# Issuing the column tiles of TensorE back to back in a two-layer diffusion trunk

## The chip, the cores and the metric

The kernel runs on one core of one Trainium2 chip. The metric is device time in microseconds (us) of one launch; lower is better. Times of a kernel are given as the median of several runs, and one further execution was taken with the hardware profiler.

## What is computed

Two layers of a hybrid trunk over 512 latent tokens and 256 context tokens of width 1024, all in float32. Cut to what matters here:

```python
for l in range(DEPTH):                                   # DEPTH = 2
    mod   = silu(c)     @ w_mod[l] + b_mod[l]            # w_mod[l]: 1024 x 6144, two rows only
    mod_c = silu(c_ctx) @ w_mod[l] + b_mod[l]
    h, hc = modulate(rmsnorm(x), ...), modulate(rmsnorm(ctx), ...)
    # one projection of h and hc; its columns feed two groups of heads:
    #   (A) 8 heads of a bidirectional gated delta rule in chunks of 64, latent scans start
    #       from the final context state; a triangular system is solved for every chunk
    #   (B) 8 heads of latent attention over all latent and all context keys
    y = concat(A, B) @ w_out[l];  x = x + g1 * y
    x = x + g2 * swiglu(modulate(rmsnorm(x), ...))       # hidden width 2816
    # the same for ctx in layer 0
return rmsnorm(x)
```

Attention of group B is `softmax(q k^T) v` for 512 queries and 768 keys per head.

## The kernel before, in words

**Products.** Activations lie transposed, features on the 128 partitions and tokens along the free axis. Large products split every operand into a high and a low float32r half (`load_w`, `split`, `gemm`, L193 to L222): three matmuls of 128x512 for each 128x128 block of weights. The weights of a block are loaded by SyncE's DMA queue, rounded by ScalarE and subtracted by VectorE (L205, L206).

**Column tiles.** Three products have an output of fewer than 128 partitions, so that several of them fit side by side in TensorE's columns:

- *Modulation* (class `Mod`, L257 to L305). `Mod.unit` (L284) takes one block of 128 rows and 2048 columns of `w_mod` in four parts of 512 columns. Part j is multiplied with the two conditioning vectors, padded to 32 columns, into partitions 32j to 32j+31 of the bank `psM` (L290). A layer has 24 units of four matmuls. The first eight of layer 0 run inside `ctx_in` from tiles `g` of 1024 columns; the other sixteen run in `mod_rest(0)`. In layer 1 eight run in `ctx_in1` and sixteen in `mod_rest(1)`, all from tiles `m` of 512 columns, each with a DMA of its own (L270).
- *Values* (`attend`, L945). For a pair of heads and each of six blocks of 128 keys, the scores of head 0 and head 1 are made in a bank `psB` (L956), ScalarE takes the exponential (L961), and L965 multiplies the exponentials by the values of the head into partitions 0 to 63 or 64 to 127 of `psA`.
- *Denominators* (L972), the same with a column of ones, once for a pair of heads.

A float32 matmul shows as two records in the trace, so a unit is eight records of L290 and a value pair four of L965.

**Order of the work.** Eleven kinds of streams, written as Python generators, make the two layers: `ctx_in`, `ctx_mla`, `ctx_ffn`, `ctx_in1`, `ctx_chain` (delta rule of the context), `lat_in`, `lat_chain` (delta rule of the latents, heads 0 to 3 and then 4 to 7), `mla_prep`, `mla_att`, `mod_rest`, `lat_ffn`. `weave` (L78) takes them in turns: a stream yields its estimated length and its work on TensorE and VectorE, `paced` (L1311) multiplies these by a pace, and the stream with the earliest time and the lowest rank is next. Rank and pace of each stream stand in the table `TUNE` (L51). The order that `weave` traces sets priorities; a list scheduler then orders each engine's queue by its own estimate of when inputs are ready, and may put other work between two matmuls that stand together in the source. Each engine runs its queue strictly in that order.

**The delta rule.** `gdn_pre` (L448) solves the triangular systems on VectorE: 31 steps of a product and a subtraction (L566 to L570, seen as L139 with tiles `st` and `g`), after which TensorE joins the blocks (L582, L583, L592, L593). It runs six times: context, latent heads 0 to 3, latent heads 4 to 7, in each layer.

**Maxima.** `prep` (L899) finds the row maxima of the scores of a head with matmuls L928 and L933 and VectorE reductions L929 and L934.

Of the kernel before, what the change touches and what calls it, by code (L numbers as in the profile page):

```python
# [3 lines left out]

# [16 lines left out]
P = 128  # L21
D = 1024
KD = 8
# [25 lines left out]


TUNE = {  # L51
    ("ctx_in", 0): (3, 0.7),
    ("ctx_mla", 0): (1, 0.7),
    ("ctx_ffn", 0): (3, 0.801),
    ("ctx_in1", 0): (3, 1.0),
    ("ctx_chain", 0): (0, 1.0),
    ("mod_rest", 0): (1, 0.7),
    ("lat_in", 0): (2, 1.0),
    ("lat_chain", 0): (1, 1.0),
    ("mla_prep", 0): (4, 1.17),  # L60
    ("mla_att", 0): (5, 0.374),
    ("lat_ffn", 0): (6, 1.0),
    ("ctx_chain", 1): (0, 1.0),
    ("mod_rest", 1): (1, 1.0),
    ("lat_in", 1): (2, 1.0),
    ("lat_chain", 1): (0, 0.6),
    ("mla_prep", 1): (3, 1.5),
    ("mla_att", 1): (5, 1.0),
    ("lat_ffn", 1): (6, 1.0),
}  # L70

# [34 lines left out]
def trunk_kernel(ctx, tc, xin, cc, wmod, small, win, wuq, wuk, wuv, wout, wgu, wdn, cst, rope, out):  # L106
    nc = tc.nc
    V, A, G, PE = nc.vector, nc.scalar, nc.gpsimd, nc.tensor
# [54 lines left out]
    ones_k = cst_t[:, C_ONE:C_ONE + 1]  # L163
# [20 lines left out]
    sc = cp.tile([P, KD, 32], F32, name="sc")  # L184
# [39 lines left out]
    def gemm_f32(w, xs, o):  # L224
        for k, x_ in enumerate(xs):
            PE.matmul(o, w[:, k * P:k * P + P], x_, start=k == 0, stop=k == len(xs) - 1)  # L226

    def pipelined(items, load, use, depth=1):
        items = list(items)
        q = []  # L230
        for i in range(min(depth, len(items))):
            q.append(load(items[i]))
        for i, it in enumerate(items):
            if i + depth < len(items):
                q.append(load(items[i + depth]))
            yield use(it, q.pop(0))
# [20 lines left out]
    class Mod:  # L257
# [26 lines left out]
        def unit(self, g, k, parts):  # L284
            l = self.l
            if k == 0:
                self.ps = ps("M")
            o = self.ps
            for j in range(4):
                PE.matmul(o[32 * j:32 * j + 32, :], sc[:, k, :], parts[j],  # L290
                          start=k == 0, stop=k == KD - 1, tile_position=(0, 32 * j))
            if k < KD - 1:
                return
            rows = slot("t", w=512)
            cpy(rows, o)
            pt = ps("M")
            for i in range(4):
                PE.matmul(pt[:, 8 * i:8 * i + 8], rows[:, P * i:P * i + P], sel, start=True, stop=True)
            o = self.t[:, 16 * g:16 * g + 16, :].rearrange("p (j i) r -> p i j r", j=4)
            b = smalls[l][:, B_MOD + 16 * g:B_MOD + 16 * g + 16].rearrange("p (j i) -> p i j", j=4)  # L300
            tt(o, pt[:, 0:32].rearrange("p (i j r) -> p i j r", i=4, j=4), b.unsqueeze(3).to_broadcast([P, 4, 4, 2]), ADD)
            for i, gg, scale, gain in ((0, 0, 8, N1), (1, 2, 32, N2)):
                if gg == g:
                    ts(self.al[:, i], self.t[:, scale:scale + 8, :], 1.0, op0=ADD)
                    tt(self.al[:, i], self.al[:, i], smalls[l][:, gain:gain + KD].unsqueeze(2).to_broadcast([P, KD, 2]))  # L305
# [417 lines left out]
    v = SimpleNamespace()  # L723
    nrs = [slice(64 * hp, 64 * hp + 64) for hp in range(2)]
# [170 lines left out]
    def mla_lat(l, cqh, kvs, yt):  # L895
# [49 lines left out]
        def attend(j, s, tag):  # L945
            y = raw_tile("f") if j < 3 else slot("hd")
            py = ps(tag)
            acc = [None, None]
            for i in range(6):
                pts = []  # L950
                for hp in range(2):
                    Q, K = s["Q"][hp], s["K"][0 if i < 2 else 1][hp]
                    b = P * (i if i < 2 else i - 2)
                    pst = ps("B")
                    for cnt, (ki, qi) in enumerate(((0, 0), (0, 1), (1, 0))):
                        PE.matmul(pst, K[ki][:, b:b + P], Q[qi], start=cnt == 0, stop=cnt == 2)  # L956
                    if i == 0:
                        acc[hp] = pt = wp.tile([P, 512], F32, name=nm("acc"), tag=("fh", "fl")[hp], bufs=3)
                    else:
                        pt = slot("t", w=n)  # L960
                    act(pt, pst, AF.Exp, scale=scale)  # L961
                    pts.append(pt)
                    yield 0.75, 0.75, 0.1
                for hp in range(2):
                    PE.matmul(py[nrs[hp]], v.vt[i][:, P * j + 64 * hp:P * j + 64 * hp + 64], pts[hp], start=i == 0, stop=i == 5)  # L965
                if i:
                    for hp in range(2):
                        tt(acc[hp], acc[hp], pts[hp], ADD, e=V)
                yield 1.2, 1.2, 0.1
            pd = ps(tag)  # L970
            for hp in range(2):
                PE.matmul(pd[nrs[hp]], ones_k.to_broadcast([P, 64]), acc[hp], start=True, stop=True)  # L972
            den = slot("t", w=n)
            V.reciprocal(out=den, in_=pd)
            stt(y, den, 1.0 / D, py, MUL, MUL)
            yt.append(y)
# [468 lines left out]
```

## Time and profile before

| | |
|---|---|
| median of 3 runs | 2263.81 us (2262.18 to 2264.55) |
| the profiled execution's own time | 2268.44 us |
| its span from the first to the last instruction | 2266.4 us |
| TensorE (PE) busy | 2087.5 us, 92% of the span |
| VectorE (DVE) busy | 1495.9 us, 66% |
| ScalarE (ACT) busy | 872.6 us, 39% |
| mean granted TensorE clock | 0.954 of full speed |

PE and PEld are matmuls and weight loads of TensorE. Matmuls are pipelined, so what one costs in a stream is the distance from its start to the next start and not its duration. The chain of waits is the work that ended last, followed back from the last instruction.

### The profile page before, as it was taken

Reading aid. Unit: us, or ns where it says so; the run is one execution under the profiler, and the core shown is the slowest. Engines: PE = TensorE matmul, PEld = TensorE weight load, DVE = VectorE, ACT = ScalarE, POOL = GpSimd, SP = SyncE. Lnnn points to the kernel's source line nnn. Section 1 sums busy time; section 2 is a strip of 40 time slices with the busy share of each in tenths; the row PEclk is TensorE's granted clock in tenths of the full one; section 3 lists DMA queues with packets and bytes.
Section 4 is the critical chain, followed back from the end, with each engine's and each line's share of the span. In section 5 each row is a group of like instructions: output and inputs, shape, how many; then the busy total and the mean of one; then the engine's idle time right before and its main releaser. Section 6 shows DMA issues by size and latency. Waiting matters only on the chain.

```text
span 2266.4 us, 40584 instructions
## 1 busy us (share of the span) xinstructions
PE 2087.5 (92%) x16048; PEld 1606.8 (71%) x16048; DVE 1495.9 (66%) x2926; ACT 872.6 (39%) x1541; POOL 126.3 (6%) x283
## 2 busy tenths in 40 slices
PE   6999989889899999999999999996985998999996
PEld 3767677789895556778888886675643576888885
DVE  4779659986678667688544457797678455444445
ACT  3453365444344434452332234435332234222333
POOL 0200013000200000010000000200010000000000
PEclk9999988899999999999999999997997999999998
DMA  8335604343345401252222236621110012323332
GB/s 321 134 122 170 210 22 129 112 152 127 108 145 163 127 25 56 71 168 89 89 76 94 93 96 211 191 93 35 38 34 14 30 66 75 95 96 98 98 96 76
DMA packets 130637, 240.41 MB, mean 106 GB/s; under 512 B 15184, under 2 KB 30064, under 8 KB 130448
## 3 DMA queue, kind: packets, MB, share of 16 engines
q1 hardware_dynamic: 124592, 224.10, 30.3%
q0 software_dynamic: 5856, 13.74, 2.2%
q8 instruction: 126, 2.06, 0.4%
q14 instruction: 63, 0.52, 0.1%
HBM read 228.24 MB, written 6.91 MB: 104 GB/s over the span
## 4 chain that ended last, share of the span: by engine, by line
PE 75%; DVE 14%; DMA 4%; ACT 4%; issue 3%; SPq 0%; ACTq 0%; DVEq 0%; POOL 0%
PE psA L221 33%; PE psM L221 14%; PE psF L221 4%; PE psB L956 3%; PE psA L965 3%; PE psM L290 2%; PE psA L226 2%; PE psB L617 2%; DVE g L139 2%; PE psC L664 2%; DVE g L148 1%; DVE fl L139 1%; PE psC L676 1%; PE psC L687 1%; ACT t L151 1%
## 5 line engine op out<-in xcount | busy, mean ns | idle before, releaser
L221 PE MATMUL psA<-hx,wh 128*128 128x512 f32 x1680 | 535.7, 398 | 21.3 <-ACT hx L151 10.8
L151 ACT ACTIVATE wh<-wr 128x512 fp32r<-128x512 f32 (+2 forms) x410 | 249.1, 608 | 642.3 <-PE psA L221 458.4
L139 DVE TENSOR_TENSOR wl<-wr,wh 128x512 fp32r<-128x512 f32 (+2 forms) x410 | 270.5, 660 | 228.8 <-ACT wh L151 228.4
L221 PEld LDWEIGHTS psA<-hx,wh 128*128 128x128 f32 x1680 | 315.1, 190 | 112.6 <-ACT hx L151 14.0
L221 PE MATMUL psA<-hx,wl 128*128 128x512 f32 x840 | 332.3, 396 | 4.4 <-DVE wl L139 4.4
L221 PE MATMUL psM<-hx,wh 128*128 128x512 f32 x704 | 217.5, 390 | 0.0
L221 PEld LDWEIGHTS psA<-hx,wl 128*128 128x128 f32 x840 | 159.6, 190 | 43.2 <-DVE wl L139 6.0
L151 ACT ACTIVATE fh<-fr 128x512 fp32r<-128x512 f32 (+3 forms) x186 | 110.8, 599 | 157.0 <-PE psF L221 47.9
L139 DVE TENSOR_TENSOR fl<-fr,fh 128x512 fp32r<-128x512 f32 (+3 forms) x186 | 119.8, 650 | 53.3 <-ACT fh L151 51.3
L148 DVE SCALAR_TENSOR_TENSOR g<-psA,mod,g 128x512 f32<-128x512 f32 x112 | 83.9, 749 | 103.9 <-PE psA L221 103.3
L221 PEld LDWEIGHTS psM<-hx,wh 128*128 128x128 f32 x704 | 132.3, 188 | 27.3
L221 PE MATMUL psM<-hx,wl 128*128 128x512 f32 x352 | 137.0, 389 | 0.0
L221 PE MATMUL psF<-m,fh 128*128 128x256 f32 x600 | 116.8, 293 | 8.2 <-ACT tc L151 5.4
L221 PE MATMUL psA<-hd,wh 128*128 128x512 f32 x384 | 120.5, 392 | 0.0
L221 PEld LDWEIGHTS psF<-m,fh 128*128 128x128 f32 x600 | 95.9, 195 | 14.6 <-ACT tc L151 7.1
L221 PE MATMUL psA<-ox,wh 128*128 128x512 f32 x320 | 100.7, 393 | 0.0
L221 PE MATMUL psM<-m,fh 128*128 128x256 f32 x416 | 80.5, 291 | 8.0 <-ACT m L151 7.9
L221 PE MATMUL psF<-m,fl 128*128 128x256 f32 x300 | 86.5, 288 | 1.5 <-DVE fl L139 1.5
L151 ACT ACTIVATE t<-psB 128x512 f32<-128x512 f32 x80 | 47.7, 597 | 99.2 <-PE psB L956 74.0
L226 PE MATMUL psA<-m,g 128*128 128x256 f32 x320 | 75.6, 397 | 10.7 <-DMA g<-win 4.0
L221 PEld LDWEIGHTS psA<-hd,wh 128*128 128x128 f32 x384 | 71.7, 188 | 16.5 <-DVE hd L139 1.0
L226 PEld LDWEIGHTS psA<-m,g 128*128 128x128 f32 x320 | 63.2, 200 | 21.3 <-ACT m L151 7.6
(382 smaller groups left out, 3797.6 us busy)
## 6 DMA issues: line engine op xcount, KB each, us to landing
wr<-wgu SPq DMA_DIRECT2D x176, 256.0 KB, 2.6
m<-wmod SPq DMA_DIRECT2D x160, 256.0 KB, 4.1
fr<-wgu SPq DMA_DIRECT2D x88, 256.0 KB, 2.7
wr<-win SPq DMA_DIRECT2D x80, 256.0 KB, 3.0
wr<-wdn SPq DMA_DIRECT2D x64, 256.0 KB, 2.6
g<-win SPq DMA_DIRECT2D x20, 512.0 KB, 7.4
g<-wmod SPq DMA_DIRECT2D x16, 512.0 KB, 10.2
fr<-wdn SPq DMA_DIRECT2D x32, 256.0 KB, 2.8
```

Source lines behind the costliest of these rows:

```text
L139: (e or V).tensor_tensor(out=out, in0=a, in1=b, op=op)
L148: V.scalar_tensor_tensor(out=out, in0=a, scalar=s, in1=b, op0=op0, op1=op1)
L151: A.activation(out, a, f, **kw)
L221: PE.matmul(o, ww[:, wk], xx if n is None else xx[:, a:a + n], start=cnt == 0, stop=cnt == 3 * nk - 1)
L226: PE.matmul(o, w[:, k * P:k * P + P], x_, start=k == 0, stop=k == len(xs) - 1)
L290: PE.matmul(o[32 * j:32 * j + 32, :], sc[:, k, :], parts[j], start=k == 0, stop=k == KD - 1, tile_position=(0, 32 * j))
L617: PE.matmul(pv[s, q, d, :], u3(lh[d])[s, c, :], u3(rh[d])[s, c, :], start=True, stop=True)
L664: PE.matmul(o[s], x_[s], y_[s], start=i == 0, stop=i == len(mm) - 1)
L676: PE.matmul(v4(ws)[s, hi, d, :], v4(w)[s, hi, d, :], S[s, hi, d, :], start=True, stop=True)
L687: PE.matmul(v4(kv)[s, hi, d, :], u3(ks[d])[s, unit(hi, n, d), :], v4(u)[s, hi, d, :], start=True, stop=True)
L956: PE.matmul(pst, K[ki][:, b:b + P], Q[qi], start=cnt == 0, stop=cnt == 2)
L965: PE.matmul(py[nrs[hp]], v.vt[i][:, P * j + 64 * hp:P * j + 64 * hp + 64], pts[hp], start=i == 0, stop=i == 5)
```

## The change

Two things change. A helper `together` makes the matmuls of a group of column tiles from the last to the first, each queued on TensorE directly behind the one made before it. The edge concerns the order in TensorE's queue alone: none of them waits for another to finish. It is used for the modulation units, the value pairs and the denominator pairs. And ten of the eighteen entries of `TUNE` get other numbers, two of these in rank and pace both.

```diff
+    def together(mms):
+        prev = None
+        for mm in mms[::-1]:
+            with nullcontext() if prev is None else tc.issue_after(prev.ins):
+                prev = mm()
...
-            for j in range(4):
-                PE.matmul(o[32 * j:32 * j + 32, :], sc[:, k, :], parts[j],
-                          start=k == 0, stop=k == KD - 1, tile_position=(0, 32 * j))
+            together([partial(PE.matmul, o[32 * j:32 * j + 32, :], sc[:, k, :], parts[j],
+                              start=k == 0, stop=k == KD - 1, tile_position=(0, 32 * j)) for j in range(4)])
...
-                for hp in range(2):
-                    PE.matmul(py[nrs[hp]], v.vt[i][:, P * j + 64 * hp:P * j + 64 * hp + 64], pts[hp], start=i == 0, stop=i == 5)
+                together([partial(PE.matmul, py[nrs[hp]], v.vt[i][:, P * j + 64 * hp:P * j + 64 * hp + 64], pts[hp],
+                                  start=i == 0, stop=i == 5) for hp in range(2)])
...
-            for hp in range(2):
-                PE.matmul(pd[nrs[hp]], ones_k.to_broadcast([P, 64]), acc[hp], start=True, stop=True)
+            together([partial(PE.matmul, pd[nrs[hp]], ones_k.to_broadcast([P, 64]), acc[hp], start=True, stop=True) for hp in range(2)])
...
-    ("ctx_ffn", 0): (3, 0.801),
+    ("ctx_ffn", 0): (3, 1.003),
...
-    ("mla_prep", 1): (3, 1.5),
-    ("mla_att", 1): (5, 1.0),
+    ("mla_prep", 1): (5, 1.755),
+    ("mla_att", 1): (5, 1.07),
```

All matmuls of the three groups stand at L232 in the changed kernel, the line of `prev = mm()`; lines behind it are five or six higher than before. The number of instructions on every engine is the same.

TensorE in `mod_rest(0)`, while the latent projection L221 runs beside it; `psM` is the bank of the modulation, `m` a part of `w_mod`. Before:

```order
188 L290 MATMUL psM_1112<-m_948,sc 32x512
189 L221 MATMUL psA_1207<-hx_676,wl_1126 128x512
190 L221 MATMUL psA_1207<-hx_682,wh_1125 128x512
191 L221 MATMUL psA_1207<-hx_683,wh_1125 128x512
192 L221 MATMUL psA_1207<-hx_682,wl_1126 128x512
193 L290 MATMUL psM_1112<-m_950,sc 32x512
194 L290 MATMUL psM_1112<-m_952,sc 32x512
195 L221 MATMUL psA_1281<-hx_640,wh_1197 128x512
196 L221 MATMUL psA_1281<-hx_641,wh_1197 128x512
197 L290 MATMUL psM_1112<-m_954,sc 32x512
```

And now:

```order
136 L221 MATMUL psA_923<-hx_682,wl_908 128x512
137 L232 MATMUL psM_1020<-m_889,sc 32x512
138 L232 MATMUL psM_1020<-m_887,sc 32x512
139 L232 MATMUL psM_1020<-m_885,sc 32x512
140 L232 MATMUL psM_1020<-m_883,sc 32x512
141 L221 MATMUL psA_1045<-hx_640,wh_913 128x512
```

The four parts of a unit, which stood among projections alone or in twos, follow one another in reversed order.

TensorE in the attention of layer 1, first pair of heads; `psA_16078` before and `psA_16097` now is the output of the values, L956 (now L961) the scores, L478 and L542 (now L483 and L547) work of the delta rule. Before:

```order
6595 L965 MATMUL psA_16078<-t_16590,m_16008 64x512
6596 L941 MATMUL psA_16401<-ident_r,mneg_16399 128x128 x4
6597 L965 MATMUL psA_16078<-t_16596,m_16008 64x512
...
6608 L965 MATMUL psA_16078<-t_16628,m_16014 64x512
6609 L972 MATMUL psA_16675<-acc_16083,cst 64x512
6610 L965 MATMUL psA_16078<-t_16655,m_16014 64x512
6611 L478 MATMUL psB_16681<-cst,g_2746_14771 64x64
6612 L972 MATMUL psA_16675<-acc_16089,cst 64x512
```

And now:

```order
6598 L961 MATMUL psB_16701<-hx_15524,hx_15503 128x512
6599 L536 MATMUL psB_16784<-cst,g_3025_16559 128x2 x8
6600 L547 MATMUL psB_16794<-g_2699_14568 64x64
6601 L232 MATMUL psA_16097<-t_16705,m_16034 64x512
6602 L232 MATMUL psA_16097<-t_16663,m_16034 64x512
6603 L232 MATMUL psA_16724<-acc_16108,cst 64x512
6604 L232 MATMUL psA_16724<-acc_16102,cst 64x512
```

The two heads of a pair stand behind one another, the head whose exponential is made last in front.

VectorE at the end of the sixth triangular solve (layer 1, latent heads 4 to 7); the rows with `st` are steps of the solve, L929 and L934 (now L934 and L939) the maxima. Before:

```order
2463 L929 TENSOR_REDUCE mx_17254<-psA_17264 128x1
2464 L139 TENSOR_TENSOR st_17037<-g_3119_17026,g_3120_17027 128x112
2465 L139 TENSOR_TENSOR g_3120_17027<-g_3120_17027,st_17037 128x4x28
2466 L934 TENSOR_REDUCE mx_17254<-psA_17267 128x2
...
2475 L139 TENSOR_TENSOR g_3120_17027<-g_3120_17027,st_17037 128x31
2476 L573 STREAM_TRANSPOSE g_3118_17025<-g_3120_17027 128x32x32
```

And now:

```order
2459 L139 TENSOR_TENSOR g_3096_16949<-g_3096_16949,st_16959 128x31
2460 L578 STREAM_TRANSPOSE g_3094_16947<-g_3096_16949 128x32x32
2461 L579 STREAM_TRANSPOSE g_3095_16948<-g_3096_16949 128x32x32
2462 L934 TENSOR_REDUCE mx_17270<-psA_17271 128x1
...
2467 L939 TENSOR_REDUCE mx_17270<-psA_17287 128x2
```

The six maxima of the last head, which were spread through the last steps of the solve, follow behind its end, and the solve's last step stands sixteen rows earlier in VectorE's queue.

## Rows read from the trace of the kernel before

**Rows 1.** The page: busy us of the engines, share of the span, count.

```profile
PE 2087.5 (92%) x16048; PEld 1606.8 (71%) x16048; DVE 1495.9 (66%) x2926; ACT 872.6 (39%) x1541; POOL 126.3 (6%) x283
```

**Rows 2.** Chain of waits by line: windows 135:276, 700:760, 748:930, 1370:1446, 1537:1642, 1642:1756, 1756:1872.

```profile
by line: PE psA L221 76.4%; PE psM L290 15.1%; PE psB L542 3.8%; PE psB L531 1.3%; PE psF L330 0.9%; PE psB L370 0.7%; PE psF L221 0.6%; PE psM L298 0.6%; PE psB L417 0.3%; PE psB L397 0.2%; PE psB L399 0.2%; PE psB L398 0.2%
...
by line: PE psM L290 22.5%; PE psA L965 14.7%; PE psA L221 9.2%; PE psB L956 8.8%; DMA fr<-wdn 6.1%; PE psA L928 5.1%; DMA m<-wmod 5.0%; issue 4.6%; PE psA L972 3.3%; DVE st L139 3.2%; DVE g L139 3.2%; DVE hd L139 2.2%; PE psB L582 2.1%; PE
...
by line: PE psA L221 30.1%; PE psB L956 16.5%; PE psA L965 16.5%; PE psB L617 5.1%; PE psC L664 5.0%; PE psA L928 3.3%; PE psA L972 3.3%; PE psC L676 2.7%; PE psC L687 2.0%; PE psA L941 1.9%; DVE t L974 1.9%; DVE mx L934 1.5%; DVE g L139 1.
...
by line: PE psA L221 67.7%; PE psM L290 17.3%; DMA m<-wmod 6.4%; PE psB L330 2.6%; PE psB L370 1.4%; SPq L270 1.2%; PE psM L298 1.0%; issue 0.8%; PE psB L417 0.5%; PE psB L397 0.4%; PE psB L399 0.3%; PE psB L398 0.3%; PE psB L478 0.3%
...
by line: PE psB L956 7.9%; PE psA L965 7.5%; PE psA L928 7.1%; PE psC L664 6.8%; PE psA L221 6.5%; PE psA L779 6.1%; PE psB L617 5.9%; PE psC L676 5.3%; PE psC L687 4.6%; DVE mx L934 3.1%; DVE t L139 3.1%; PE psA L330 3.1%; DVE g L139 2.9%;
...
by line: PE psB L956 14.4%; PE psA L965 9.1%; DVE g L139 7.0%; issue 6.7%; DVE mx L929 5.9%; PE psA L928 4.9%; DVE acc L139 4.8%; DVE mx L934 4.0%; DVE st L139 3.8%; PE psA L941 3.4%; PE psA L972 3.4%; DVE t L974 2.9%; ACT t L151 2.7%; PE p
...
by line: PE psA L221 39.7%; PE psB L956 13.0%; PE psA L965 12.0%; PE psB L617 7.1%; PE psC L664 6.0%; PE psC L676 4.3%; PE psC L687 3.7%; issue 3.1%; PE psC L719 1.8%; PE psC L713 1.8%; PE psA L972 1.7%; PE psB L582 1.3%; PE psB L592 1.2%; 
```

**Rows 3.** Windows: length, busy us (count) of PE, PEld, DVE, ACT, POOL; clock, DMA.

```profile
135.00:276.00 141.00, 141.00 (x769) 97.53 (x769) 113.17 (x244) 49.89 (x94) 6.97 (x29) 0.99 0.57 189
...
748.00:930.00 182.00, 173.61 (x1549) 113.87 (x1550) 120.69 (x218) 72.34 (x130) 4.37 (x15) 0.94 0.19 60
...
1642.00:1756.00 114.00, 81.34 (x491) 45.19 (x490) 94.33 (x191) 34.57 (x59) 12.94 (x15) 0.87 0.08 24
1756.00:1872.00 116.00, 111.04 (x1338) 79.93 (x1338) 60.78 (x110) 36.89 (x61) 0.00 (x0) 0.95 0.14 49
```

**Rows 4.** Timeline of PE near 151 us: start, length, line, output, form, count.

```profile
150.84 1.05 PE L290 MATMUL psM<-m,sc 128*32 128x512 f32 x4
151.82 0.73 PE L221 MATMUL psA<-hx,wh 128*128 128x512 f32 x2
```

**Rows 5.** Timeline of PE near 720 us.

```profile
719.73 0.40 PE L928 MATMUL psA<-hd,hd 128*128 128x512 f32 x1
719.96 0.39 PE L956 MATMUL psB<-hx,hx 128*128 128x512 f32 x1
720.28 1.06 PE L290 MATMUL psM<-m,sc 128*32 128x512 f32 x8
721.28 1.07 PE L965 MATMUL psA<-t,m 128*64 128x512 f32 x2
722.28 0.50 PE L928 MATMUL psA<-hd,hd 128*128 128x512 f32 x1
722.62 0.87 PE L956 MATMUL psB<-hx,hx 128*128 128x512 f32 x3
```

**Rows 6.** Timeline of weight loads (PEld): one whole unit near 246 us.

```profile
246.37 0.16 PEld L290 LDWEIGHTS psM<-m,sc 128*32 128x32 f32 x8 [0.35 <-DVE g L139]
```

**Rows 7.** Timeline of PE at the first eight units; in brackets idle time and its end.

```profile
17.89 1.05 PE L290 MATMUL psM<-g,sc 128*32 128x512 f32 x4 [0.24 <-DMA g<-wmod]
```

**Rows 8.** Chain of waits near 1742 us in order of time: start, length, what.

```profile
1742.12 0.81 PE psA L928
1742.96 0.70 DVE mx L929
1743.70 0.81 PE psA L928
...
1753.24 3.01 issue
```

**Rows 9.** Lines L290, then L965: idle time of TensorE before them, times.

```profile
  DMA m<-wmod: 15.3, 18
...
  ACT t L151: 11.5, 19
```

**Rows 10.** The page: exponentials of the scores on ScalarE; landing of the modulation's parts.

```profile
L151 ACT ACTIVATE t<-psB 128x512 f32<-128x512 f32 x80 | 47.7, 597 | 99.2 <-PE psB L956 74.0
...
m<-wmod SPq DMA_DIRECT2D x160, 256.0 KB, 4.1
```

More of the change, by code (lines that the diff above doesn't have):

```diff
@@ L1 @@
-from contextlib import ExitStack
+from contextlib import ExitStack, nullcontext
 from functools import partial
@@ L51 @@
 TUNE = {
-    ("ctx_in", 0): (3, 0.7),
-    ("ctx_mla", 0): (1, 0.7),
-    ("ctx_ffn", 0): (3, 0.801),
-    ("ctx_in1", 0): (3, 1.0),
+    ("ctx_in", 0): (3, 0.749),
+    ("ctx_mla", 0): (3, 0.7),
+    ("ctx_ffn", 0): (3, 1.003),
+    ("ctx_in1", 0): (2, 1.0),
     ("ctx_chain", 0): (0, 1.0),
     ("mod_rest", 0): (1, 0.7),
-    ("lat_in", 0): (2, 1.0),
+    ("lat_in", 0): (2, 0.595),
     ("lat_chain", 0): (1, 1.0),
-    ("mla_prep", 0): (4, 1.17),
+    ("mla_prep", 0): (4, 1.064),
     ("mla_att", 0): (5, 0.374),
     ("lat_ffn", 0): (6, 1.0),
-    ("ctx_chain", 1): (0, 1.0),
+    ("ctx_chain", 1): (2, 0.85),
     ("mod_rest", 1): (1, 1.0),
-    ("lat_in", 1): (2, 1.0),
+    ("lat_in", 1): (1, 1.0),
     ("lat_chain", 1): (0, 0.6),
-    ("mla_prep", 1): (3, 1.5),
-    ("mla_att", 1): (5, 1.0),
+    ("mla_prep", 1): (5, 1.755),
+    ("mla_att", 1): (5, 1.07),
     ("lat_ffn", 1): (6, 1.0),
```

## The prediction

> **What bounds the kernel now.** I began with the page: TensorE is busy for 2087.5 of 2266.4 us, VectorE for 1495.9 [rows 1]. So TensorE is the bound over the whole, but not everywhere, and the chain of waits says where. From 135 to 276 us all of the chain is TensorE's (the first line of [rows 2]), TensorE is busy for 141.00 of 141.00 us and VectorE for 113.17 [rows 3]: whatever leaves TensorE's queue there shortens the run. From 748 to 930 us it is nearly so, 173.61 of 182 us. In layer 1 between 1642 and 1756 us it is not: VectorE is busy for 94.33 of 114 us and TensorE for 81.34, since the triangular solve, the maxima and the sums of the exponentials share VectorE there (the sixth line of [rows 2]), and the granted clock falls to 0.87 while it is 0.99 in the first stretch [rows 3].
>
> **What a column tile costs.** A lone modulation matmul and a whole unit can be compared directly. One unit's half, four records, starts at 150.84 and the next matmul at 151.82: 0.98 us [rows 4]. A whole unit, eight records, starts at 720.28 and the next at 721.28: 1.00 us [rows 5]. So four column tiles that stand together run in the time of one or two. A value pair's half costs the same 1.00 us (721.28 to 722.28). I call such a run of different column tiles, with nothing between them, a round: it costs 1.0 us, whatever it holds. Beside this, TensorE pays for changing shape: two full-width matmuls start 0.23 us apart (719.73 to 719.96), but 0.32 us pass before a round (719.96 to 720.28) and 0.34 after one (722.28 to 722.62), so about 0.10 us a change.
>
> The page "TensorE: Matmul & The Clock Gate" of the Trainium skill (Part 3, The mechanism) says that a weight load overlaps with matmuls in flight only when its row group differs; column tiles all use the same rows, so by that rule a unit's loads would wait in turn and a group would gain little. The row decides otherwise: the eight loads of a whole unit lie within 0.16 us [rows 6], and by it the sum below stands, where by the rule it would be near nothing.
>
> **What the change removes.** In TensorE's queue before, the 192 modulation matmuls make 69 rounds, the 96 value matmuls 74 and the 16 denominators 9; now 49, 49 and 8. So 152 rounds become 106: 46 fewer at 1.0 us, 46 us. Changes of shape between neighbours in the queue fall from 640 to 585, which is 55 at 0.10 us, 5.5 us. TensorE loses 51.5 us of work, 1.12 us a round. What of it lies on the path goes by place:
>
> - `mod_rest(0)`, 27 rounds to 16: 11 at 1.12 is 12.3 us. It lies in the stretch that is TensorE's alone, and 113 us of VectorE's work fit into the 129 that stay. I count 11, since a unit's last parts must still land.
> - The eight units in `ctx_in1`, 14 to 9: 5.6 us. Around them the modulation is 22.5% of the chain, but landings of `wdn` and `wmod` are 11% (the second line of [rows 2]). I count 4.
> - Values and denominators of layer 0, 38 to 28: 11.2 us. TensorE is busy for 95% of that stretch, and the values are 16.5% of the chain. I count 9.5.
> - `mod_rest(1)`, 20 to 16: 4.5 us, with 6.4% of the chain a wait for `wmod` (the fourth line of [rows 2]). I count 3.
> - Values and denominators of layer 1, 45 to 29: 17.9 us. On the chain are values for 7.5% of 105, 9.1% of 114 and 12.0% of 116 us and denominators for 3.4% of 114 and 1.7% of 116 (the last three lines of [rows 2]): 38 of some 45 us. But where VectorE is the close second a shorter TensorE queue only uncovers it, so I count 0.6 of it, 10.7.
>
> That is 38 us. The first eight units gain nothing: each waits for its DMA [rows 7], and the group now waits for the later of two.
>
> **What the other order moves.** The new table moves little: between the same landmarks (the six solves, the two feed-forward stages) TensorE's and VectorE's queues hold the same work as before but for the rounds. From layer 0's output projection to the start of layer 1 (930 to 1370 us) and from layer 1's output projection to the end nothing changes, so I count 0 there. Two moves matter. The solve of latent heads 0 to 3 in layer 0 starts 32 rows earlier in VectorE's queue and ends six rows later; six rows of about 0.7 us are at most 4 us, and the context's feed-forward covers them while it has TensorE's chain, so 0; without that cover it is 4. In layer 1 the six maxima of the last head go behind the solve. They now alternate with TensorE on the chain, 0.81 and 0.70 us, 1.58 us a step [rows 8], six times, some 9 us in front of the solve's end. Behind it they lie beside the joining of the blocks, where the chain stands for 3.01 us in issue anyway. I count 5 of the 9, for the products behind must wait for the reductions in turn; the bounds are 0 and 9.
>
> Sum: 38 and 5 make 43 us less. The profiled execution's own time was 2268.44, so it would be 2225; the median lies 4.6 us under it, at 2263.81, and so I forecast **2221 us** for the median.
>
> **The rivals.**
>
> *Half of it is hidden.* If VectorE, the DMA landings and the new order eat what TensorE gives back in all places but the two that are TensorE's alone (11 and 9.5 us), 20 us remain: 2244. For it speaks that VectorE is busy for four fifths of 135 to 276 and of 1642 to 1756 us; against it that the chain names the removed lines themselves with 15 to 22% in three of the windows.
>
> *All of it and more.* The full 51.5 us, and 9 us from the maxima, would give 2203. For it speaks that a shorter value stretch also lets the reductions start earlier, since they alternate with it on TensorE.
>
> *Groups wait for their latest input, and the run is slower.* TensorE's queue is strict. A value pair now starts only when both exponentials are there, 0.60 us each on ScalarE, and a unit only when all four parts have landed, 4.1 us each from issue [rows 10]; before, the first part ran while the next was on its way. Everything behind the group waits too. There are 40 units outside the start and 56 value and denominator groups. The 43 us are lost at 0.45 us a group. If each pair waited one exponential (34 us) and each unit 1 us more (40 us), the run would end 31 us later, at 2295. For it speaks that L290 already waits for DMA 15.3 us in 18 times and L965 for exponentials 11.5 us in 19 [rows 9]. Against it: in the new queue score matmuls and delta-rule products stand between the last score of a pair and its values, and the parts are requested a unit ahead.
>
> *The tiles stand together and still take turns.* Then only the order changes: 2264, no change. Against it speak, plainly, [rows 5, 6]. The rule of the Trainium skill named above speaks for it.
>
> **How the numbers follow.** A measurement of this kernel tells about 0.2%, 4.5 us, from no change. I give my forecast, between 2211 and 2236, 0.50; half hidden, 2236 to 2257, 0.22; more than all, under 2211, 0.14; groups that wait, slower by over 4.5 us, 0.08; the tiles in turns, 0.02, and waits that just balance the gain, 0.04. The range that leaves out no more than 2 in 10 goes from 2203, the full sum with 9 us of the maxima, to 2250. Faster is 0.50 and 0.22 and 0.14, that is 0.86; same 0.06; slower 0.08.
>
> **What would show it.** Right: L232 has 49, 49 and 8 rounds that begin together; the busy time of PE falls by about 45 to 50 us; layer 1's output projection starts about 40 us earlier, and the distance from there to the end stays within 2 us of what it is; the stretch with `mod_rest(0)` shortens by about 11 us with PE still busy throughout. Half hidden would show as the same fall of busy time with more idle time on PE, ended by VectorE or DMA. The slower rival would show as waits of L232 for `ACT t` and `DMA m<-wmod` well above the present 27 us together. I would be wrong altogether if records of one group started 0.4 us apart instead of a few ns, or if the stretch between layer 0's attention and layer 1 changed by more than 5 us, for then the new order would have moved what I took as fixed.

## The result, and the profile after

The changed kernel took 2234.02 us in the median of 4 runs (2228.82 to 2237.56), the kernel before 2264.18 in 4 runs beside it: a ratio of 0.9859 with an interval from 0.983 to 0.9889, 30 us less. The forecast was 2221 and its range held the time. The profiled execution of the changed kernel took 2228.82, the shortest of its four; between the two profiled executions the difference is therefore larger, 39.6 us, and the views below show that larger one.

The page, busy us of the engines (answers to [rows 1]):

```profile
PE 2034.1 (91%) x16048; PEld 1592.5 (72%) x16048; DVE 1497.3 (67%) x2926; ACT 871.5 (39%) x1541; POOL 127.1 (6%) x283
```

TensorE is busy for 53.4 us less, the other engines for the same. The forecast of this number was 45 to 50. To see where it became time, both spans are cut at the same three places: the start of the norm behind layer 0's output projection, the first norm of layer 1, and the norm in front of layer 1's feed-forward. Columns as in [rows 3]. Before:

```profile
0.00:930.20 930.20, 853.84 (x7711) 658.46 (x7712) 676.08 (x1429) 401.74 (x752) 74.45 (x171) 0.95 0.40 132
930.20:1370.80 440.60, 431.20 (x2785) 354.70 (x2783) 264.42 (x485) 161.75 (x280) 13.69 (x31) 0.98 0.32 101
1370.80:1871.50 500.70, 435.72 (x3963) 295.09 (x3963) 366.55 (x728) 181.41 (x305) 38.14 (x81) 0.92 0.24 75
1871.50:2266.40 394.90, 366.78 (x1593) 298.51 (x1591) 188.84 (x285) 127.69 (x205) 0.00 (x0) 0.97 0.28 91
```

After:

```profile
0.00:893.30 893.30, 812.19 (x7711) 645.88 (x7712) 675.01 (x1429) 401.25 (x751) 74.48 (x171) 0.95 0.42 137
893.30:1331.10 437.80, 428.90 (x2791) 352.54 (x2789) 264.25 (x485) 161.77 (x280) 13.68 (x31) 0.99 0.32 102
1331.10:1832.30 501.20, 425.74 (x3960) 295.14 (x3957) 369.35 (x728) 180.95 (x305) 38.94 (x81) 0.88 0.24 75
1832.30:2227.00 394.70, 367.30 (x1593) 298.94 (x1591) 188.69 (x285) 127.56 (x205) 0.00 (x0) 0.97 0.28 91
```

Nearly all of the gain lies in the first row: 36.9 us. The second and the fourth became shorter by 2.8 and 0.2. The third is the lesson of this case. Layer 1 lost 20 of the 46 rounds, some 22 us of TensorE's work at the forecast's price, and became 0.5 us longer. Its TensorE is busy for only 10.0 us less, at a granted clock of 0.88 where it was 0.92, and idle (length less busy) for 75.5 us where it was 65.0. What the removed rounds gave there turned about half into idle time and half into slower matmuls.

That the groups themselves do what they say is plain from TensorE's timeline after, a unit near 130 us and value pairs near 711 us:

```profile
130.32 1.06 PE L232 MATMUL psM<-m,sc 128*32 128x512 f32 x8
131.31 0.49 PE L221 MATMUL psA<-hx,wh 128*128 128x512 f32 x1
...
711.04 2.10 PE L232 MATMUL psA<-t,m 128*64 128x512 f32 x8
713.07 0.50 PE L933 MATMUL psA<-g,hd 128*128 128x512 f32 x1
```

A unit of eight records takes 0.99 us to the next start; two value pairs, eight records, take 2.03. One round costs 1.0 us, as [rows 4, 5] said.

The waits show the price. TensorE's waits, after (what waited, for what; us in total, times, longest):

```profile
PE psM L232 <- DMA m<-wmod: 11.7, 6, 3.6
PE psM L232 <- DMA g<-wmod: 7.0, 7, 1.5
```

Before, the same two lines, at L290:

```profile
PE psM L290 <- DMA m<-wmod: 3.7, 4, 2.6
PE psM L290 <- DMA g<-wmod: 2.5, 11, 0.2
```

So units now wait 12.5 us longer for `w_mod`: 8.0 in the units from tiles `m`, and 4.5 in the first eight. These 4.5 cost nothing: the first unit begins at 12.8 us where it began at 11.5, but the eighth begins at 30.4, and before the second half of the eighth began at 30.7. A group cannot start before its last part has landed, while the first part alone used to run ahead. In the wider count of [rows 9], everything that ended the idle time before L232:

```profile
  DMA m<-wmod: 28.3, 16
...
  ACT t L151: 9.6, 18
```

against 15.3 and 11.5 us, 13.0 more and 1.9 less. The exponentials cost nothing more; the landings do. The dearest of these waits also shows what comes on top (TensorE's timeline after, in brackets the idle time before; under it the window of that unit):

```profile
1341.97 1.93 PE L232 MATMUL psM<-m,sc 128*32 128x512 f32 x8 [2.19 <-DMA m<-wmod]
1343.83 1.65 PE L221 MATMUL psA<-hx,wh 128*128 128x512 f32 x3
```

```profile
1341.90:1343.80 1.90, 1.83 (x8) 0.20 (x8) 1.90 (x4) 0.92 (x2) 0.00 (x0) 0.50 1.05 389
```

The unit takes 1.86 us instead of 0.99, at a granted clock of 0.50, the lower of the two levels, 1.2 GHz. In `mod_rest(1)` four rounds fewer were worth 3 us by the forecast; the stretch from the first of its sixteen units to the ninth, which holds the four, took 62.7 us before (1369.8 to 1432.5) and takes 63.0 after (1330.1 to 1393.1).

### The profile page after: what moved, and what is told of

It is laid out like the page before. It is cut to its first block, busy times and chain, and to the rows that moved or that the text cites. A ratio compares the mean times of both kernels' runs of the same rounds, so it can differ in the third digit from the quotient of the medians.

```text
span 2227.0 us, 40577 instructions
## 1 busy us (share of the span) xinstructions
PE 2034.1 (91%) x16048; PEld 1592.5 (72%) x16048; DVE 1497.3 (67%) x2926; ACT 871.5 (39%) x1541; POOL 127.1 (6%) x283
## 5 line engine op out<-in xcount | busy, mean ns | idle before, releaser
L221 PE MATMUL psA<-hx,wh 128*128 128x512 f32 x1680 | 535.0, 398 | 20.2 <-ACT hx L151 8.5
L221 PEld LDWEIGHTS psA<-hx,wh 128*128 128x128 f32 x1680 | 314.5, 190 | 107.6 <-issue 12.4
L221 PE MATMUL psA<-hx,wl 128*128 128x512 f32 x840 | 330.7, 394 | 5.3 <-DVE wl L139 5.3
L221 PE MATMUL psM<-hx,wh 128*128 128x512 f32 x704 | 217.6, 390 | 0.0
L221 PEld LDWEIGHTS psA<-hx,wl 128*128 128x128 f32 x840 | 159.0, 189 | 42.2 <-DVE wl L139 8.3
L148 DVE SCALAR_TENSOR_TENSOR g<-psA,mod,g 128x512 f32<-128x512 f32 x112 | 83.9, 749 | 105.8 <-PE psA L221 105.6
L221 PEld LDWEIGHTS psM<-hx,wh 128*128 128x128 f32 x704 | 132.3, 188 | 27.2
L139 DVE TENSOR_TENSOR fl<-fr,fh 128x512 fp32r<-128x512 f32 (+3 forms) x186 | 120.5, 653 | 39.2 <-ACT fh L151 37.7
L221 PE MATMUL psM<-hx,wl 128*128 128x512 f32 x352 | 137.0, 389 | 0.0
L221 PE MATMUL psF<-m,fh 128*128 128x256 f32 x600 | 117.3, 294 | 6.5 <-ACT tc L151 5.0
L221 PE MATMUL psA<-hd,wh 128*128 128x512 f32 x384 | 120.4, 392 | 0.0
L221 PEld LDWEIGHTS psF<-m,fh 128*128 128x128 f32 x600 | 96.2, 195 | 13.0 <-ACT tc L151 6.6
L221 PE MATMUL psA<-ox,wh 128*128 128x512 f32 x320 | 100.7, 393 | 0.0
L221 PE MATMUL psF<-m,fl 128*128 128x256 f32 x300 | 86.8, 289 | 4.4 <-DVE fl L139 4.2
L221 PEld LDWEIGHTS psA<-hd,wh 128*128 128x128 f32 x384 | 71.7, 188 | 16.4 <-DVE hd L139 1.1
L221 PE MATMUL psM<-m,fh 128*128 128x256 f32 x416 | 81.3, 293 | 1.6 <-ACT m L151 0.9
L221 PEld LDWEIGHTS psM<-hx,wl 128*128 128x128 f32 x352 | 66.1, 188 | 13.6
```

Of the source, the lines that this page charges most:

```text
L139: (e or V).tensor_tensor(out=out, in0=a, in1=b, op=op)
L148: V.scalar_tensor_tensor(out=out, in0=a, scalar=s, in1=b, op0=op0, op1=op1)
L221: PE.matmul(o, ww[:, wk], xx if n is None else xx[:, a:a + n], start=cnt == 0, stop=cnt == 3 * nk - 1)
```

## The experiments

The change has two halves, so the first question was which one pays. "Rounds" are counted in TensorE's queue as in the prediction, modulation, values and denominators; before 69, 74 and 9, after 49, 49 and 8. For each kernel stand the median, the runs, and the ratio to the kernel before with its interval.

**The groups with the old table.** The change, with all entries of `TUNE` as before:

```diff
-    ("ctx_in", 0): (3, 0.749),
-    ("ctx_mla", 0): (3, 0.7),
+    ("ctx_in", 0): (3, 0.7),
+    ("ctx_mla", 0): (1, 0.7),
...
```

> The column tiles grouped, the table of ranks and paces as before. Rounds in TensorE's queue: 49, 49 and 8, as in the change. If the removed rounds carry the gain (theory A) it runs in 2224 to 2230 us, 34 to 40 us under before, so as fast as the change or faster. If the new table carries a good half of it (theory B), 2245 to 2252. If the new numbers of layer 1 cost what the groups bring there (theory C), the stretch from the end of the sixth solve to the output projection of layer 1 is near before's 115 us and not the 124 us of the change.

Measured: 2252.98 (6 runs), 0.9935, 0.9914 to 0.9956; rounds 49, 49 and 8. The same 46 rounds are gone as in the change and only 14 us are gained, a little less than theory B had. The stretch of theory C is short again: 112.8 us from the end of the sixth solve's transposes (1741.1 us) to the norm in front of the feed-forward (1853.9), where the change takes 123.7 and the kernel before 115.3.

**The new table without the groups.** The three calls of `together` become the loops of before again; one of them:

```diff
-            together([partial(PE.matmul, pd[nrs[hp]], ones_k.to_broadcast([P, 64]), acc[hp], start=True, stop=True) for hp in range(2)])
+            for hp in range(2):
+                PE.matmul(pd[nrs[hp]], ones_k.to_broadcast([P, 64]), acc[hp], start=True, stop=True)
```

> The new table, no groups: 65, 72 and 10 rounds against 69, 74 and 9 before. Theory A: 2258 to 2268, no change that can be told. Theory B: 2244 to 2250. Theory C: slower than before in layer 1 by 5 to 10 us, because the six maxima of the last head stand behind the sixth solve, and faster in layer 0 by as much.

Measured: 2269.42 (11 runs), 1.0011, 1.0001 to 1.0021; rounds 65, 72 and 10. The table alone is worth nothing; if anything it costs 2 us. Theory B is out. Layer 1 is 3.6 us longer (1367.8 to 1872.1, 504.3 us, against 500.7), on the side that theory C said and below its 5 to 10; layer 0 is no faster. So the two halves are not added: −14 and +2 would make −12, and together they make −30. TensorE's idle time shows where most of the rest is. The first stretch, up to the norm behind layer 0's output projection, with the groups and the old table, then with the new table alone:

```profile
0.00:919.60 919.60, 827.23 (x7710) 658.09 (x7711) 675.65 (x1429) 401.06 (x751) 73.69 (x171) 0.93 0.42 133
```

```profile
0.00:929.90 929.90, 848.88 (x7710) 659.43 (x7711) 675.63 (x1429) 402.13 (x751) 73.16 (x171) 0.94 0.41 132
```

TensorE's idle time there is 76.4 us in the kernel before and 92.4 with the groups in the old order, but 81.0 with the new order alone and 81.1 with both (82.2 to 86.8 in three further kernels below with both). In the old order the groups open 16 us of gaps, in the new order 0 to 6. What in the order does this, no run shows.

**Which numbers of the table.** Groups with the new numbers of layer 0 and the old ones of layer 1, and the other way round:

```diff
-    ("ctx_chain", 1): (2, 0.85),
+    ("ctx_chain", 1): (0, 1.0),
...
-    ("mla_prep", 1): (5, 1.755),
-    ("mla_att", 1): (5, 1.07),
+    ("mla_prep", 1): (3, 1.5),
+    ("mla_att", 1): (5, 1.0),
```

> Groups, the new numbers of layer 0, the old ones of layer 1. Theory C: 2222 to 2228, 6 to 12 us under the change, with the maxima back inside the sixth solve. If VectorE's work hides what layer 1's groups remove whatever the order (theory D), it equals the change, 2230 to 2238.

> Groups, the old numbers of layer 0, the new ones of layer 1. Theory C: 6 to 12 us over the kernel with groups and the old table, the maxima behind the sixth solve and over 120 us from there to layer 1's output projection. Theory D: equal to it within 4 us.

Measured: layer 0's numbers 2232.92 (4 runs), 0.9848, 0.9832 to 0.9865, the whole change. Layer 1's numbers 2255.32 (6 runs), 0.9948, 0.9933 to 0.9964, no better than the groups with the old table. Both agree with theory D. In the kernel with layer 0's numbers five of the six maxima of the last head stay inside the sixth solve, and it is as fast as the change: their move gains nothing.

The windows of layer 1 add to this. Four kernels have the groups and the old numbers of layer 1, and the same order of TensorE's queue there (the groups with the old table, the one with layer 0's numbers, and the two below that split these); three have the order of the change there (the change, the one with layer 1's numbers alone, and the one below that asks for two units ahead). From the first norm of layer 1 to the norm in front of its feed-forward the four take 492.9, 495.3, 498.9 and 500.8 us, on average 497.0, and the three 501.2, 500.7 and 503.1, on average 501.7. The shortest of the four, the groups with the old table:

```profile
1361.00:1853.90 492.90, 419.02 (x3961) 293.06 (x3958) 366.35 (x728) 180.91 (x306) 38.69 (x81) 0.90 0.25 76
```

With 500.7 for the kernel before and 504.3 for the new table alone, the groups bring 3.7 us in layer 1 with its old numbers and 2.6 with the new, and the new numbers cost 3.6 without groups and 4.7 with them. These are single executions, and the four spread over 8 us.

Layer 0's numbers were then split: groups with new numbers for `ctx_in`, `ctx_mla` and `lat_in` alone, and for `ctx_ffn`, `ctx_in1` and `mla_prep` alone. On the change, for the first of the two:

```diff
-    ("ctx_ffn", 0): (3, 1.003),
-    ("ctx_in1", 0): (2, 1.0),
+    ("ctx_ffn", 0): (3, 0.801),
+    ("ctx_in1", 0): (3, 1.0),
...
-    ("mla_prep", 0): (4, 1.064),
+    ("mla_prep", 0): (4, 1.17),
```

> Groups, the old table but for ctx_in, ctx_mla and lat_in of layer 0: 48, 49 and 8 rounds. If the gain of the new numbers with groups comes from where the modulation of layer 0 stands among the projections (up to 310 us), this alone brings 2236 to 2242, against 2253 to 2255 with the old table; if it comes from the context's feed-forward beside the attention (310 to 930 us), it stays at 2248 to 2256.

> Groups, the old table but for ctx_ffn, ctx_in1 and mla_prep of layer 0: 52, 49 and 8 rounds. The other half: 2236 to 2242 if the feed-forward and the preparation of the attention carry the gain, 2250 to 2258 if the first numbers do.

Measured: the first three 2243.64 (6 runs), 0.9913, 0.9893 to 0.9933; the other three 2262.09 (12 runs), 0.9986, 0.9967 to 1.0004. Neither lies in a range that was expected. Beside the groups alone, the first three give 9 us, the others alone take away 9, and both give 20 (by the ratios to the kernel before 5, 12 and 20). So the numbers belong together, and why they do is not settled: in the stretch up to the output projection TensorE is idle for 88.6 us with the first three and 96.5 with the others, and the waits behind it are small and differ from one kernel to the next.

**Which groups.** In the new order, only the value and denominator pairs grouped, then only the modulation units:

```diff
-            together([partial(PE.matmul, o[32 * j:32 * j + 32, :], sc[:, k, :], parts[j],
-                              start=k == 0, stop=k == KD - 1, tile_position=(0, 32 * j)) for j in range(4)])
+            for j in range(4):
+                PE.matmul(o[32 * j:32 * j + 32, :], sc[:, k, :], parts[j],
+                          start=k == 0, stop=k == KD - 1, tile_position=(0, 32 * j))
```

> The new table; only the value and denominator pairs are grouped, the modulation is not: 62, 50 and 8 rounds, so 27 fewer than with the new table alone. If each removed round brings its price wherever it stands (theory A), 20 to 30 us under the new table alone, 2240 to 2249. If the modulation groups are what gains and the pairs only uncover VectorE's work (theory B), 2258 to 2266.

> The new table; only the modulation is grouped: 49, 73 and 10 rounds, 16 fewer than with the new table alone. Theory A: 13 to 18 us under it, 2251 to 2256. If a group of four parts gives back in waits for its last landing what it saves (theory W), 2260 to 2268, with TensorE idle for the parts of the modulation some 12 us as in the whole change, against 5.

Measured: values alone 2252.76 (4 runs), 0.9941, 0.9918 to 0.9964, rounds 62, 50 and 8; modulation alone 2253.72 (6 runs), 0.9947, 0.993 to 0.9963, rounds 49, 73 and 10. The first lies between the two theories, the second where theory A put it, although TensorE waits 13.8 us for the parts of the modulation. Against the new table without groups that is 17 us for 27 rounds and 16 us for 15, together 32 of the 35 that the change has over that kernel. So the gain is the removed rounds, and it adds up within one order of the queues. A round of the modulation is worth about its full 1.0 us, one of the values some 0.6; by the intervals each of the two differences is uncertain by 5 to 6 us. The windows show where it comes from; the stretch up to the output projection and layer 1's up to its feed-forward norm, with the values grouped, then with the modulation:

```profile
0.00:914.50 914.50, 830.68 (x7710) 651.57 (x7711) 676.64 (x1429) 402.51 (x751) 73.15 (x171) 0.95 0.42 134
1354.00:1855.20 501.20, 431.37 (x3964) 296.73 (x3964) 369.28 (x728) 180.75 (x306) 39.33 (x81) 0.88 0.25 75
```

```profile
0.00:911.20 911.20, 827.08 (x7710) 651.87 (x7711) 675.69 (x1429) 401.57 (x751) 74.08 (x171) 0.95 0.42 134
1350.50:1855.00 504.50, 438.94 (x3961) 296.21 (x3958) 367.80 (x728) 181.04 (x306) 39.27 (x81) 0.90 0.24 74
```

With the new table alone these stretches took 929.9 and 504.3 us. The values bring 15.4 us in layer 0 and 3.1 in layer 1; the modulation 18.7 and nothing.

**Is it the landings?** If groups lose by waiting for their last part, asking for the parts earlier should give it back. The change, with the parts of two units requested ahead instead of one in the two stretches of 16 units:

```diff
-            parts = self.load(*todo[0], tag)
+            ahead = 2 if n == 16 else 1
+            parts = [self.load(*u, tag) for u in todo[0:ahead]]
...
-                nxt = self.load(*todo[i + 1], tag) if i + 1 < n else None
+                if i + ahead < n:
+                    parts.append(self.load(*todo[i + ahead], tag))
...
```

> The change, with the parts of the modulation requested two units ahead instead of one in the two stretches of sixteen units. Theory W: TensorE's idle time for them falls from 11.7 us to under 6, and the run is 2224 to 2230 us, 5 to 9 us under the change. If other work waits in their place (the same DMA engines, the buffers of the ring), 2231 to 2238 as the change, with the waits shifted to the projection's weights.

Measured: 2235.23 (4 runs), 0.9866, 0.9839 to 0.9892, and the wait is as long as it was:

```profile
PE psM L232 <- DMA m<-wmod: 12.5, 6, 4.2
```

But the edit did not make the requests earlier. Three of the six waits lie in the eight units of `ctx_in1`, which it leaves as they were. The parts of the other three units (the last of `mod_rest(0)`, the fourth and fifth of `mod_rest(1)`) are requested 10.1, 7.4 and 7.6 us before the unit begins in the change, and 10.3, 8.0 and 7.8 us before it here. The kernel has 12 tiles `m`, which hold the parts of three units, and in `mod_rest(1)` the fourth unit's parts are requested only when the first unit has used its own. That unit begins at 1330.15 us in the change and at 1338.02 here; SyncE's timeline, the change, then here:

```profile
1331.22 2.62 SPq L276 DMA_DIRECT2D m<-wmod  x4
```

```profile
1339.10 1.91 SPq L276 DMA_DIRECT2D m<-wmod  x4
```

So theory W was not tested: what an earlier request would be worth stays open. In the window of the waiting unit above, the DMA engines have no share left either (1.05, 389 GB/s); that was seen in this one unit.

**Why layer 1 gains next to nothing: the clock?** Its matmuls run at 0.88. If the lower clock were the cause, work that keeps TensorE busy where it waits anyway would pay. Two more matmuls follow each of 32 matmuls for the maxima in layer 1; their results are not read and the output is unchanged.

```diff
+                    if l:
+                        keep = ps("M")
+                        for _ in range(2):
+                            PE.matmul(keep, Q[hp][0][:, P * qi:P * qi + P], kl, start=True, stop=True)
```

> The change, with two extra matmuls of the same operands into an unread bank behind each of the 32 matmuls of the maxima in layer 1; the output stays the same. Theory K: the lower granted clock eats what the groups save in layer 1; the clock rises from 0.75 to over 0.9 from the fifth solve's end to the sixth's, and the run is 2222 to 2230 us although it has 16 us more of work. If the clock is only a result of TensorE waiting for VectorE, the extra work shows as 2236 to 2246.

Measured: 2243.76 (4 runs), 0.99, 0.9881 to 0.9919, some 10 us slower than the change. The two stretches in front of the joining of the sixth solve (L582 before), in the change, then here:

```profile
1496.00:1590.40 94.40, 79.39 (x1175) 56.42 (x1176) 68.60 (x141) 39.22 (x69) 8.17 (x21) 0.83 0.13 34
1590.40:1708.70 118.30, 79.92 (x485) 47.59 (x485) 95.70 (x196) 35.52 (x61) 14.13 (x15) 0.75 0.09 28
```

```profile
1503.00:1604.20 101.20, 87.36 (x1210) 61.48 (x1210) 70.97 (x146) 39.70 (x69) 8.12 (x21) 0.89 0.12 32
...
1604.20:1720.40 116.20, 84.15 (x513) 50.26 (x512) 92.68 (x192) 35.61 (x61) 13.30 (x15) 0.82 0.10 28
```

The clock rises from 0.83 to 0.89 and from 0.75 to 0.82, and yet the first stretch is 6.8 us longer and the second only 2.1 shorter. Clock that is bought with work does not pay for it here. The 0.9 that theory K asked for was not reached, so what a higher clock without added work would be worth stays open. In the second stretch VectorE is busy for 95.70 of 118.30 us and TensorE for 79.92; that VectorE's work is the limit there is argued from this and not shown.

**Why layer 1 gains next to nothing: the bank of the maxima?** TensorE waits there for reductions to free a bank. Every second matmul for the maxima of layer 1 goes to the bank `psM`, which the modulation has left; first on the change, then on the kernel with layer 1's old numbers. The scheduler also moves some 200 of the 3960 records of TensorE in layer 1, so bank and order change together.

```diff
-                    p = ps(tag)
+                    p = ps("M" if l and qi % 2 else tag)
...
-                    p = ps(tag)
+                    p = ps("M" if l and qi else tag)
```

> The change, with every second matmul of the maxima in layer 1 written to the bank of the modulation, which is free there, so that the maxima use a bank more. If the alternation of these matmuls with VectorE's reductions holds what the groups save in layer 1 (theory M), TensorE's waits for the reductions in layer 1 fall from 16 us to under 8, layer 1 up to its output projection takes 492 us or less where the change has 502, and the run is 2220 to 2228 us. If VectorE's own work is the limit (theory D), the waits move and the run stays at 2230 to 2238.

> The same bank, on the kernel with groups, the new numbers of layer 0 and the old ones of layer 1. Theory M: 2218 to 2226 us, 8 to 14 under that kernel. Theory D: 2229 to 2237.

Measured: on the change 2237.28 (4 runs), 0.9885, 0.9868 to 0.9903, no gain. With layer 1's old numbers 2224.93 (2222.06 to 2225.01, 4 runs), 0.9824, 0.9809 to 0.9839: faster than both kernels, by the medians 9 us under the change, though the two intervals still touch. Layer 1 of this kernel, and of the one with the same order but without the bank:

```profile
1340.70:1824.70 484.00, 412.44 (x3961) 290.21 (x3958) 367.15 (x728) 180.88 (x306) 38.59 (x81) 0.90 0.25 78
```

```profile
1345.50:1844.40 498.90, 425.90 (x3960) 298.45 (x3957) 366.69 (x728) 181.29 (x305) 38.78 (x81) 0.88 0.25 75
```

Fifteen us less, nearly all of it busy time of TensorE and hardly any idle time (71.6 and 73.0). That overstates it: the profiled execution without the bank took 2241.85 us, the longest of its four and 9 above their median. Against the 497.0 us that four kernels with its order take on average, the bank is worth 13 us in this stretch, and by the medians 8. Nearly all of the 13 lie in front of the end of the sixth solve's transposes, which comes 368.9 us behind the first norm where it is 378.2 to 383.5 in the four. TensorE's largest wait for a reduction in layer 1, without the bank, then with it:

```profile
PE psA L933 <- DVE mx L934: 7.4, 8, 1.4
```

```profile
PE psA L938 <- DVE mx L934: 1.5, 2, 1.1
```

So layer 1 takes 484.0 us where the kernel before took 500.7. Whether its removed rounds are paid out by this, or the bank would bring as much without groups, is not shown: the kernel before was not run with the bank. With the new numbers of layer 1 the same bank is worth nothing by the medians (498.4 us for the stretch, against 501.7). That the bank was one of the limits in the old order fits these numbers, but the waits became shorter and TensorE's idle time did not; why its busy time fell instead, and what limits the new order, the runs do not tell.

## Why the prediction was right and where it was wrong

**The rounds.** Right. A round costs 1.0 us whatever it holds, 46 rounds and 55 changes of shape were to take 51.5 us off TensorE, and its busy time fell by 53.4. The rule of the Trainium skill ("TensorE: Matmul & The Clock Gate", Part 3, The mechanism), by which a weight load overlaps only where its row group differs, would have left 2264 as the prediction applied it; the runs with one kind of group each (17 and 16 us) speak against it for these column tiles. Another page of the Trainium skill, "TensorEngine Tiling (Array Packing)", Key Properties, has tiles load and multiply side by side, and the rows agree: the four tiles of a unit take 0.99 us together.

**Layer 0.** The forecast counted 11, 4 and 9.5 us, 24.5. The profiled execution shows 36.9, but that is one execution: four more kernels have the same order of TensorE's queue up to layer 0's output projection (layer 1's numbers old, the two with the bank, the one with more matmuls) and reach it at 906.1, 901.7, 898.1 and 901.2 us. The mean of the five is 900.1, 30 us under the one execution of the kernel before (and under the 929.9 of the new table alone), about the full price of the 26 rounds removed there, 29 us. So this term was too small by about 5, near the size of the spread: with the new table the deductions for landings and for VectorE were not needed. The sign named for `mod_rest(0)` came out in part. TensorE is no longer busy throughout (126.11 of the 130 us from 123 to 253), and the last of its sixteen units begins at 273.0 us where it began at 280.7. But with the groups and the old table it begins at 280.5, and with the new table alone at 273.3: by this mark the table gained there and not the groups, although TensorE had been busy for 141.00 of 141.00 us.

**What makes it so** was not seen at all. The prediction said that the new table "moves little" and gave its layer 0 part no weight. The groups in the old order keep only some 13 of these 30 us (919.6 and 914.3 us in the two kernels that have it), and layer 0's numbers decide over 20 of the medians. The forecast had laid 38 us to the groups and 5 to the table; alone they bring 14 and −2. That it came out near is luck: both halves were changed at once, and each needs the other.

**Layer 1.** This is the step that failed. For `mod_rest(1)` the forecast counted 3 and for values and denominators 10.7, "0.6 of it"; for the maxima 5. Measured for all three: 0.5 us lost between two profiled executions. By the averages above the groups brought some 3 us instead of the 13.7 of the first two terms, and the new numbers, with the maxima behind the solve, cost some 4 where 5 were to be gained. The prediction named the reason itself, "a shorter TensorE queue only uncovers it", and then took six tenths all the same; the chain's shares of 7.5 to 12% for the values were read as time that would vanish. The maxima are seen best in VectorE's timeline at the end of the sixth solve, before (start, length, what):

```profile
1752.19 0.19 DVE L139 TENSOR_TENSOR g<-g,st 128x31 f32<-128x31 f32 x1
...
1754.20 1.95 DVE L574 STREAM_TRANSPOSE g<-g 128x1024 f32<-128x1024 f32 x1
1762.10 1.23 DVE L139 TENSOR_TENSOR g<-g,eghx 128x1024 f32<-128x1024 f32 x1 [5.95 <-PE psB L593]
1763.25 1.40 DVE L148 SCALAR_TENSOR_TENSOR g<-psB,cst,g 128x512 f32<-128x512 f32 x2
```

and after:

```profile
1704.67 0.19 DVE L139 TENSOR_TENSOR g<-g,st 128x31 f32<-128x31 f32 x1
...
1706.68 1.93 DVE L579 STREAM_TRANSPOSE g<-g 128x1024 f32<-128x1024 f32 x1
1708.49 0.65 DVE L934 TENSOR_REDUCE mx<-psA 128x1 f32<-128x512 f32 x1
1710.42 0.69 DVE L934 TENSOR_REDUCE mx<-psA 128x1 f32<-128x512 f32 x1 [1.27 <-PE psA L933]
...
1716.92 0.69 DVE L939 TENSOR_REDUCE mx<-psA 128x2 f32<-128x512 f32 x1 [0.94 <-PE psA L938]
...
1717.90 0.75 DVE L148 SCALAR_TENSOR_TENSOR g<-psB,cst,g 128x512 f32<-128x512 f32 x1
```

Before, 7.1 us lie between the end of the transposes (1756.15) and L148, 5.95 of them idle. After, six reductions stand in that gap, each but the first waiting 0.9 to 1.3 us for its matmul, and L148 starts 9.3 us behind the transposes (1708.61 to 1717.90). Counted from layer 1's first unit the solve's last step does end earlier, after 374.8 us instead of 382.6, 7.8 of the 9 us that were its upper bound. The new table alone does as much: the transposes end 376.6 us behind the first norm of layer 1 with it, 377.5 in the change and 385.4 before. But the joining gives 2 back at once, and the stretch behind it the rest: 123.6 us at a clock of 0.91, where it took 115.2 us at 0.96 (the last line of [rows 3] has nearly the same stretch).

```profile
1708.70:1832.30 123.60, 117.91 (x1364) 84.99 (x1365) 66.36 (x119) 38.31 (x64) 0.00 (x0) 0.91 0.13 45
```

TensorE is busy for 117.91 of it: what VectorE no longer had to wait for, TensorE had still to do. The 5 us should have been 0 or less.

**The rivals.** Groups that wait for their latest input were the slower rival, with 74 us of waits as its price. The mechanism is there at a tenth to a fifth of that: 8 to 13 us more for the tiles `m`, none for the exponentials, and 4.5 at the start that moved nothing behind it. The prediction had it as a rival only; a part of it belonged into the sum. "Half hidden", 2244, was about right in kind for layer 1, where nearly all of it is hidden, and wrong for layer 0 with the new table, where nothing is.

**What stayed fixed.** From layer 0's output projection to layer 1 the length changed by 2.8 us, under the 5 that would have upset the argument, and the tail by 0.2. The forecast of 40 us at layer 1's output projection became 39.2 at the norm behind it, though from other parts: layer 0 about 5 more than counted, layer 1 about 19 less, and the rest is the spread of single executions.

In all: 43 us were forecast and 30 measured. The missing 13 are layer 1's 18.7, less the 5 that layer 0 gave beyond its count.

## What to carry to other kernels

Column tiles that stand side by side in TensorE's queue share one pass, so count rounds and not matmuls, and price a removed round by the stretch it is in: here about the full price in layer 0, where TensorE is nearly the only bound, but under half of it with a table that does not fit (13 of 29 us), and some 3 of 22 us in layer 1, where VectorE is the close second. A group starts when its last input is there, so put the longest of its inputs' waits into the sum. An order of the queues found for one set of groups does not carry over: table and groups were worth +2 and −14 us alone and −30 together, and a change of one is tested with the other fitted to it.

## What the runs showed that was not expected

- One order of TensorE's queue up to layer 0's output projection, profiled executions of kernels that differ only behind it: 893.3, 898.1, 901.2, 901.7 and 906.1 us, at granted clocks of 0.95, 0.94, 0.94, 0.95 and 0.93. One order of it in layer 1: 492.9 to 500.8 us, at 0.90 to 0.88. A single profile can't place a gain of 10 us in this kernel.
- A wait in front of a group can be paid twice: 2.19 us of waiting, and then 1.86 us for a unit that otherwise takes 0.99, because the granted clock was 0.50.
- Sixty-four unread matmuls in layer 1 raised the clock of a waiting stretch from 0.75 to 0.82 and made it 2 us shorter, but lengthened the stretch before it by 7.
